# Low-rank gate logits as one fp32r product of stacked parts, and other places and banks for the transposes of the second seam half

## The chip, the cores and the metric

The kernel runs on one core of a Trainium2 chip. The core has five engines with instruction queues of their own: TensorE (PE; its weight loads are listed as PEld), VectorE (DVE), ScalarE (ACT), GpSimd (POOL) and SyncE (SP), which here issues the DMAs. An engine takes its instructions in order and waits at semaphores for the others. The metric is the device time of one execution in microseconds (us); lower is better.

## The reference, cut to what matters

One layer of a hybrid decoder: a gated DeltaNet branch A and a gated linear attention branch B (GLA), merged by gates, an output projection, and an MLP with a squared ReLU. 1024 tokens, model width 1024, all in float32. The two places that the change touches:

```python
h = rms_norm(x, norm_mix_pre[l])
proj = h @ w_in[l]                    # ..., a_b, a_a (4 columns each), ..., b_glr (16 columns), ...
# branch B: decay of each of 512 key channels, from a rank-16 input
gate_logit = gate_lr @ gate_w2 + gate_b
log_a = log_sigmoid(gate_logit) / 16
...
merged = sigmoid(gate_a) * y_a + sigmoid(gate_b) * y_b
x = x + rms_norm(merged @ w_o[l], norm_mix_post[l])
h = rms_norm(x, norm_mlp_pre[l])
u = square(relu(h @ w_mlp_up[l]))
x = x + rms_norm(u @ w_mlp_down[l], norm_mlp_post[l])
```

## The kernel before

**Precision.** Nearly every large product is made of fp32r matmuls. An operand is split into a leading part, rounded to fp32r by a ScalarE copy, and a trailing part, which VectorE makes by subtracting (`split`, L237). A product is then three matmuls: leading by leading, leading by trailing, trailing by leading (`mm3`). Some small products stay in plain float32.

**Stages in order.** A prologue normalises x and writes its transpose as hT and hL. Then comes the DeltaNet stage (pool `cv`), the GLA stage (pool `gl`), the merge of the two branches (pool `mp`), the output projection with the start of the MLP (pool `op`; called the seam below), the MLP's up projection (pool `ml`) and its down projection (pool `dn`). In the first two stages a function `drive` writes down TensorE's order: a main list of large products, and lanes of small jobs that are put in when a clock `T.t`, counted up by every matmul's columns, has reached their time. `TensorClock` (L57 on) counts a plain float32 matmul as four times an fp32r one. The order on the other engines is set by a scheduler with priorities; `tc.high_priority` moves instructions forward.

**Weights** come in slabs of 256 KB. Each is loaded into one of four buffers `w` of the pool `wraw` and split into `wh` and `wl`, of which there are three each.

**The low-rank path.** `decays` computes 24 narrow columns of the projection: 8 for the DeltaNet's beta and decay, 16 for the gate input. Their weights `wx` are held as 128 columns with zeros between: leading parts at columns 0 to 7 and 32 to 47, trailing parts 64 columns further. The result, 112 rows of 1024 tokens, is copied to `sm` in float32. `decays2` transposes rows 0 to 71 of it and computes the DeltaNet's decays. In the GLA stage `gw2` holds gate_w2 twice, at rows 32 to 47 and 96 to 111, zeros elsewhere, and `ball_pair` makes the logits of two heads with four plain float32 products of 128x512 over these 112 rows, into the banks t, l, r, o; there are two such pairs. A linear scan over the logits' log-sigmoid follows.

**PSUM** has four large banks (`gbank`, tag g) and four more with the tags t, l, r, o (`mbank`).

**The seam.** `merged @ w_o` runs in two halves u of 512 tokens, each with two column blocks c of 8 steps (kt). After a half, four row tiles i are normalised one after the other: VectorE writes xt (residual), ScalarE squares it, GpSimd forms the scale rs, VectorE writes m. `turn(u, i)` transposes row tile i in two groups of four and writes parts of the MLP's input: for u = 0 the blocks X11 and X21 and their splits; for u = 1 it writes X12, x22, the split R22, and sums for a Strassen-like scheme of seven products (T1, T2, and what T3 and T4 are made of). In the list of operations the X blocks carry the name `wu`, since they live in buffers of that tag, and T1 to T4 the name `big`.

The turns of u = 0 stand between the steps of the second half's projection (after the steps `TURNS[0]`, counted c * 8 + kt). Those of u = 1 stand in the loop after it, which computes products P1 and P2 of the first eight MLP blocks from the first half alone: 16 steps of 12 matmuls into the banks r and o; a turn comes after each of the steps `TURNS[1]`. Behind this loop `prep(0)` loads weights (L1073) into the buffer that X12 had, T3 and T4 are split, and `early(0)` runs the products P6 (with T2), P7 (T3), P5 (T1), P4 (T4) and P3 of block 0. P6 needs a sum of the weights that prep(0) loads.

```python
TURNS = (2, 5, 6, 9), (3, 6, 10, 12)
...
if step in TURNS[1]:
    turn(1, TURNS[1].index(step))
```

Of the kernel before, what the change touches and what calls it, by code (L numbers as in the profile page):

```python
# [7 lines left out]
F32 = mybir.dt.float32  # L8
F32R = mybir.dt.float32r
U32 = mybir.dt.uint32  # L10
AF = mybir.ActivationFunctionType
ALU = mybir.AluOpType
# [4 lines left out]
P = 128  # L17
S = 1024
# [5 lines left out]
TAU = 16.0  # L24
DFF = 4096
NE = 8
TURNS = (2, 5, 6, 9), (3, 6, 10, 12)
HP = 2000
HPX = 600
HPE = 2000  # L30
# [103 lines left out]
def kernel(  # L134
# [4 lines left out]
    w_mlp_up, w_mlp_down, out, dbg=None,  # L139
):  # L140
    nc = tc.nc
    V, A, G, T, SP = nc.vector, nc.scalar, nc.gpsimd, TensorClock(nc.tensor), nc.sync
# [6 lines left out]
    wraw = ctx.enter_context(tc.tile_pool(name="wraw", bufs=4))  # L149
# [4 lines left out]
    def gbank():  # L154
        return psg.tile([P, 512], F32, tag="g", name="g")
# [3 lines left out]
    def mbank(tag=None):  # L159
        if tag is None:  # L160
            tag = "tlro"[mturn[0] % 4]
            mturn[0] += 1
        return psm.tile([P, 512], F32, tag=tag, name="m" + tag)

    def tt(out, a, b, op, eng=None):
        (eng or V).tensor_tensor(out=out, in0=a, in1=b, op=op)  # L166
# [10 lines left out]
    def act(out, a, func, **kw):  # L177
        A.activation(out=out, in_=a, func=func, **kw)  # L178
# [15 lines left out]
    ident = const.tile([P, P], F32, name="ident")  # L194
# [131 lines left out]
    sgp = tc.alloc_tile_pool(name="sgp", bufs=2, reuse_waits="tile")  # L326
    gp = tc.alloc_tile_pool(name="gp", bufs=1, reuse_waits="tile")

    sm = gp.tile([112, S], F32, name="sm")
    bt = gp.tile([P, NTOK, 8], F32, name="bt")  # L330


# [6 lines left out]
    with tc.tile_pool(name="xp", bufs=3) as xp:  # L339
        pre = []  # L340
        for t in range(NTOK):
# [11 lines left out]
            for g in range(2):  # L353
                pt = mbank()
                for k in range(4):
                    T.transpose(out=pt[:, k * P:(k + 1) * P], in_=xn[:, (g * 4 + k) * P:(g * 4 + k + 1) * P],
                                identity=ident)
# [23 lines left out]
    def decays(cv):  # L381


        ws = cv.tile([P, KT, 24], F32, name="ws", tag="Xc")
        SP.dma_start(out=ws[:, :, 0:8], in_=win[:, :, C_AB:C_AB + 8])
        SP.dma_start(out=ws[:, :, 8:24], in_=win[:, :, C_GLR:C_GLR + 16])
        wx = cv.tile([P, KT, P], F32R, name="wx", tag="Ai", bufs=1)
        with tc.high_priority(offset=HP):
            V.memset(wx.bitcast(F32), 0.0)
            for c, r, n in ((0, 0, 8), (8, 32, 16)):  # L390
                wv = ws[:, :, c:c + n]
                A.copy(out=wx[:, :, r:r + n], in_=wv)
                tt(wx[:, :, r + 64:r + 64 + n], wv, wx[:, :, r:r + n].bitcast(F32), ALU.subtract)
        for u in range(2):
            us = slice(u * 512, u * 512 + 512)
            ps = gbank()
            for kt in range(KT):
                T.matmul(ps, wx[:, kt, :], hT[:, kt, us], start=kt == 0, stop=False)
                T.matmul(ps, wx[:, kt, :], hL[:, kt, us], start=False, stop=kt == KT - 1)
                yield  # L400
            A.copy(out=sm[:, us], in_=ps[0:112, :])

    def decays2():
        for g in range(2):
            yield LAT
            pb = mbank("tl"[g])[:, 0:288].rearrange("p (t c) -> p t c", c=72)
            for t in range(4):
                T.transpose(out=pb[:, t, :], in_=sm[0:72, (g * 4 + t) * P:(g * 4 + t + 1) * P], identity=ident[0:72, 0:72])
            V.tensor_copy(out=bt[:, g * 4:g * 4 + 4, :], in_=pb[:, :, 0:8])
            tt(bt[:, g * 4:g * 4 + 4, :], pb[:, :, 64:72], bt[:, g * 4:g * 4 + 4, :], ALU.add)  # L410
        btb = bt[:, :, 0:4].rearrange("p t h -> p h t")
        bta = bt[:, :, 4:8].rearrange("p t h -> p h t")
        act(beta, btb, AF.Tanh, scale=0.5)
        ts(beta, beta, 0.5, ALU.mult, 0.5, ALU.add)
        tt(yv, bta, bc(dtb, NTOK), ALU.add)
        act(u_, yv, AF.Abs)
        act(u_, u_, AF.Exp, scale=-1.0)
        ts(s_, u_, 2.0, ALU.add)
        V.reciprocal(out=s_, in_=s_)
        tt(s_, s_, u_, ALU.mult)  # L420
        s2 = u_
        tt(s2, s_, s_, ALU.mult)
        ts(pl, s2, 2.0 / 17, ALU.mult, 2.0 / 15, ALU.add)
        for c in (13, 11, 9, 7, 5, 3, 1):
            tt(pl, pl, s2, ALU.mult)
            ts(pl, pl, 2.0 / c, ALU.add)
        tt(pl, pl, s_, ALU.mult)
        ts(yv, yv, 0.0, ALU.max)
        tt(gr, yv, pl, ALU.add)
        tt(gr, gr, bc(nea, NTOK), ALU.mult)  # L430
        grf = gr.rearrange("p h t -> p (h t)")
        yield 10.0
        pg = mbank("t")
        T.matmul(pg[:, 0:32], upper, grf, start=True, stop=True)
        T.matmul(pg[:, 32:64], ones, grf, start=True, stop=True)
        gcf = gc.rearrange("p h t -> p (h t)")
        V.tensor_copy(out=gcf, in_=pg[:, 0:32])
        act(eg, gc, AF.Exp)
        tt(ef, pg[:, 32:64].rearrange("p (h t) -> p h t", t=NTOK), gc, ALU.subtract)
        ts(ef, ef, 0.0, ALU.min)  # L440
        act(ef, ef, AF.Exp)
        act(egl, pg[:, 32:64].rearrange("p (h t) -> p h t", t=NTOK), AF.Exp)
        yield LAT
        pgt = mbank("l")
        T.transpose(out=pgt[0:32, 0:P], in_=gcf, identity=ident)
        grow = wraw.tile([P, 2, 256], F32, tag="w", name="w")[0:32, 0, 0:P]
        V.tensor_copy(out=grow, in_=pgt[0:32, 0:P])
        SP.dma_start(out=d_g, in_=grow)
# [331 lines left out]
    with tc.tile_pool(name="gl", bufs=1, reuse_waits="tile") as gl:  # L780

        reserve(gl, (("gq", 512, 3), ("gk", 512, 3), ("gvh", S, 3), ("gvl", S, 3), ("gr", S, 4)))
        gw2 = gl.tile([112, 512], F32, name="gw2")
        V.memset(gw2, 0.0)
        for r in (32, 96):
            SP.dma_start(out=gw2[r:r + 16, :], in_=gla_gate_w2[0])
        smask = gl.tile([P, 8, 64], F32, name="smask")
        V.memset(smask, 1.0)
        V.memset(smask[:, :, 0:1], 0.0)
# [7 lines left out]
        def ball_pair(hh):  # L797

            lap = ball.rearrange("p h (u i) -> p (h u) i", u=2)
            for n in range(4):  # L800
                h, u = hh + n // 2, n % 2
                yield LAT
                gbias = chan[:, 48 + h:49 + h]
                pl_ = mbank("tlro"[n])
                T.matmul(pl_, gw2[:, h * P:(h + 1) * P], sm[:, u * 512:u * 512 + 512], start=True, stop=True)
                ts(lap[:, n, :], pl_, gbias, ALU.add, 0.0, ALU.min)
                act(e1s[:, n, :], pl_, AF.Abs, bias=gbias)
            act(e1s, e1s, AF.Exp, scale=-1.0)
            act(e1s, e1s, AF.Ln, bias=1.0)
            tt(e1s, lap, e1s, ALU.subtract)  # L810
            for n in range(4):
                V.tensor_tensor_scan(out=lap[:, n, :], data0=smask.rearrange("p c i -> p (c i)"), data1=e1s[:, n, :],
                                     initial=0.0, op0=ALU.mult, op1=ALU.add)
# [156 lines left out]
        for h in range(H):  # L970
            if h % 2 == 0:
                jobs.append(("b%d" % h, [], lambda mark, h=h: ball_pair(h)))
            jobs.append(("m%d" % h, [("v%d" % h, 2.0), ("k%d" % h, 2.0), ("b%d" % (h // 2 * 2), BW if h % 2 == 0 else 0)],
                         lambda mark, h=h: gla_mix(h, mark)))
# [15 lines left out]
    with tc.tile_pool(name="mp", bufs=1, reuse_waits="tile") as mp:  # L990
# [22 lines left out]
        for c in range(4):  # L1013
# [12 lines left out]
            for b in range(2):  # L1026
                for u in range(2):
                    us = slice(u * 512, u * 512 + 512)
# [61 lines left out]
    with tc.tile_pool(name="op", bufs=1, reuse_waits="tile") as op:  # L1090
# [12 lines left out]
        def turn(u, i):  # L1103
            m = msu[u][i]
            il = slice(i * P, i * P + P)
            pv = []
            for g in range(2):
                pt = mbank("tl"[g])
                for k in range(4):
                    T.transpose(out=pt[:, k * P:(k + 1) * P], in_=m[:, (g * 4 + k) * P:(g * 4 + k + 1) * P],  # L1110
                                identity=ident)
                pv.append(pt.rearrange("p (k c) -> p k c", c=P))
            if u == 0:
                for g, n in enumerate(("11", "21")):
                    A.copy(out=X[n][:, :, il], in_=pv[g])
                    hilo(R[n], k4, il, X[n][:, :, il])
            else:
                x11, x21, x12, x22 = (X[n][:, :, il] for n in ("11", "21", "12", "22"))
                A.copy(out=x12, in_=pv[0])
                tt(x22, pv[1], x12, ALU.subtract)  # L1120
                hilo(R["22"], k4, il, pv[1])
                tt(x12, x12, x11, ALU.subtract)
                tt(x11, x22, x11, ALU.add)
                hilo(T2, k4, il, x11)
                hilo(T1, k4, il, x12)
                tt(x21, x21, x11, ALU.subtract)

        for u in range(2):
# [4 lines left out]
            for c in range(2):  # L1133
                banks = [gbank() for _ in range(4)]
                cs = slice(c * 512, c * 512 + 512)
                for kt in range(KT):
                    hi, lo = load_slab512(wov[:, kt, cs], wsp, "w")
                    for i in range(4):
                        il = slice(i * P, i * P + P)
                        mm3(banks[i], mg_[u][0][:, kt, il], mg_[u][1][:, kt, il], hi, lo, kt == 0, kt == KT - 1)  # L1140
                    if u and c * KT + kt in TURNS[0]:
                        turn(0, TURNS[0].index(c * KT + kt))
                with tc.high_priority(offset=HPE):
# [6 lines left out]
            for i in range(4):  # L1150
                t = u * 4 + i
# [84 lines left out]
    with tc.tile_pool(name="ml", bufs=1, reuse_waits="tile") as ml:  # L1236
# [147 lines left out]
        for n in range(NU):  # L1384
# [18 lines left out]
            else:  # L1403
                if n == NU - 1:

                    r = [hp2.tile([P, 8, 512], F32, tag=t, name="r" + t) for t in ("R11", "R21")]
# [131 lines left out]
```

## Time and profile before

| | us |
|---|---|
| median of 3 runs | 1704.4 (1701.24 to 1704.83) |
| the profiled execution | 1699.28 |
| its span in the trace | 1697.5 |

| engine | busy us in the span |
|---|---|
| PE / PEld | 1653.0 / 1403.0 |
| DVE | 987.2 |
| ACT | 771.5 |
| POOL | 135.9 |

On the time axis of the trace the first gate products run at 439.8 us, the second pair's at 647.8, the seam's P1 and P2 steps from 1060.7 on, and P6 of block 0 from 1116.85.

How to read it: a stretch row gives the busy time of each engine in it, with the number of instructions in brackets. In the chain each line is a piece of the work that ended last, with its start and length. In a timeline a bracket at the end of a row tells how long the engine had been idle before it and what released it. A matmul's listed duration overlaps that of the next one, so the pace is read from starts.

### The profile page before, as it was taken

The numbers are of one execution on the slowest core, as the hardware profiler recorded it, in microseconds if no ns is written. First come the engines' busy times: TensorE is split into PE (matmuls) and PEld (weight loads), VectorE is DVE, ScalarE is ACT, GpSimd is POOL, SyncE is SP. The second block draws the span as 40 slices with busy tenths as digits, with TensorE's granted clock in tenths as the row PEclk, the third lists the DMA queues.
The fourth block names the chain that finished last, engine by engine and source line by source line (L and its number), as shares of the span: only waits on it lengthen the run. The fifth ranks groups of instructions, "written<-read, shape, count | busy, mean of one in ns | idle before, by whom it ended". The sixth has DMA issues, their size and how long they took to land.

```text
span 1697.5 us, 24475 instructions
## 1 busy us (share of the span) xinstructions
PE 1653.0 (97%) x9174; PEld 1403.0 (83%) x9174; DVE 987.2 (58%) x1678; ACT 771.5 (45%) x1576; POOL 135.9 (8%) x222
## 2 busy tenths in 40 slices
PE   7999999999999999999999999989999999999997
PEld 6888778878898989998888888778888878888886
DVE  5677565872445335643354545798777655564764
ACT  5456554643533335433421235654555555443442
POOL 3010111111001000001100011200000000000021
PEclk9999999999999999999999999999999999999999
DMA  5222213322211212122743345687678698786763
GB/s 168 56 73 76 84 38 90 92 59 67 79 45 38 69 43 58 38 63 87 235 150 97 111 159 174 212 263 231 205 258 281 240 334 307 243 272 221 249 224 136
DMA packets 186405, 251.39 MB, mean 148 GB/s; under 512 B 23351, under 2 KB 108430, under 8 KB 186286
## 3 DMA queue, kind: packets, MB, share of 16 engines
q1 hardware_dynamic: 186286, 249.83, 45.7%
q8 instruction: 72, 1.18, 0.3%
q14 instruction: 47, 0.39, 0.1%
HBM read 185.79 MB, written 63.98 MB: 147 GB/s over the span
## 4 chain that ended last, share of the span: by engine, by line
PE 82%; DVE 7%; DMA 4%; ACT 4%; issue 2%; POOL 1%; SPq 0%; DVEq 0%; ACTq 0%; POOLq 0%
PE g L68 58%; PE mr L68 8%; PE mo L68 7%; PE ml L68 4%; PE mt L68 3%; DMA gb<-d_g 2%; DVE Xt L166 1%; PE mt L72 1%; DVE Xi L548 1%; DVE wl L166 1%; ACT E L178 1%; DMA oraw<-d_oa 1%; ACT wh L237 0%; DMA rv<-in_w_mlp_down_dram 0%; ACT Zp L604 0%
## 5 line engine op out<-in xcount | busy, mean ns | idle before, releaser
L166 DVE TENSOR_TENSOR wl<-w,wh 128x512 fp32r<-128x512 f32 x181 | 125.6, 695 | 223.5 <-ACT wh L237 220.0
L68 PE MATMUL g<-hT,wh 128*128 128x512 f32 (+1 forms) x600 | 239.1, 399 | 1.2 <-DVE gr L175 0.9
L68 PE MATMUL g<-hL,wh 128*128 128x512 f32 (+1 forms) x600 | 232.8, 388 | 0.0
L68 PE MATMUL g<-hT,wl 128*128 128x512 f32 (+1 forms) x600 | 232.1, 387 | 0.0
L237 ACT CAST wh<-w 128x512 fp32r<-128x512 f32 x184 | 113.8, 619 | 208.0 <-PE g L68 175.0
L68 PE MATMUL g<-wh,hT 128*128 128x256 f32 x640 | 185.7, 290 | 0.0
L68 PE MATMUL g<-wl,hT 128*128 128x256 f32 x640 | 182.1, 284 | 0.0
L68 PE MATMUL g<-wh,hL 128*128 128x256 f32 x640 | 182.0, 284 | 0.0
L68 PE MATMUL g<-big 128*128 128x512 f32 x768 | 175.3, 389 | 1.7 <-ACT big L1231 1.6
L68 PEld LDWEIGHTS g<-big 128*128 128x128 f32 x768 | 144.0, 188 | 32.3 <-ACT big L1231 2.0
L166 DVE TENSOR_TENSOR big<-ru,big 128x1024 fp32r<-128x1024 f32 x53 | 64.9, 1225 | 114.6 <-ACT big L1231 114.2
L68 PEld LDWEIGHTS g<-hT,wl 128*128 128x128 f32 x600 | 113.4, 189 | 21.6 <-DVE wl L166 0.2
L68 PEld LDWEIGHTS g<-hT,wh 128*128 128x128 f32 x600 | 113.4, 189 | 21.5 <-DVE gr L175 1.1
L68 PEld LDWEIGHTS g<-hL,wh 128*128 128x128 f32 x600 | 113.8, 190 | 18.8 <-issue 1.0
L1231 ACT CAST big<-ru 128x1024 fp32r<-128x1024 f32 x53 | 55.8, 1053 | 153.1 <-PE g L68 56.6
L68 PEld LDWEIGHTS g<-wh,hT 128*128 128x128 f32 x640 | 123.1, 192 | 1.4 <-issue 1.0
L68 PEld LDWEIGHTS g<-wl,hT 128*128 128x128 f32 x640 | 123.2, 193 | 1.2 <-issue 1.0
L68 PEld LDWEIGHTS g<-wh,hL 128*128 128x128 f32 x640 | 123.1, 192 | 0.1
L68 PE MATMUL g<-wh,big 128*128 128x512 f32 x256 | 81.1, 393 | 0.2 <-DVE m L166 0.2
L68 PE MATMUL g<-big,wh 128*128 128x512 f32 x256 | 78.8, 389 | 0.0
L178 ACT ACTIVATE c<-c 128x512 f32<-128x512 f32 x104 | 64.1, 630 | 21.8 <-DVE c L166 20.1
L166 DVE TENSOR_TENSOR big<-rv,big 128x1024 fp32r<-128x1024 f32 x53 | 64.6, 1218 | 0.2
(450 smaller groups left out, 3377.1 us busy)
## 6 DMA issues: line engine op xcount, KB each, us to landing
ru<-d_u SPq DMA_DIRECT2D x53, 512.0 KB, 4.6
w<-in_w_in_dram SPq DMA_DIRECT2D x80, 256.0 KB, 2.7
rv<-in_w_mlp_down_dram SPq DMA_DIRECT2D x37, 512.0 KB, 5.4
wu<-in_w_mlp_up_dram SPq DMA_DIRECT2D x32, 512.0 KB, 5.6
d_u<-c SPq DMA_DIRECT2D x56, 256.0 KB, 2.9
d_u<-us SPq DMA_DIRECT2D x48, 256.0 KB, 3.3
us<-in_w_mlp_down_dram SPq DMA_DIRECT2D x48, 256.0 KB, 4.4
xt<-in_x_dram SPq DMA_DIRECT2D x16, 512.0 KB, 5.4
```

The lines of the kernel that those rows point to most:

```text
L68: return self.eng.matmul(out, lhsT, rhs, start=start, stop=stop, skip_group_check=more)
L72: return self.eng.transpose(out=out, in_=in_, identity=identity)
L166: (eng or V).tensor_tensor(out=out, in0=a, in1=b, op=op)
L178: A.activation(out=out, in_=a, func=func, **kw)
L237: A.copy(out=hi, in_=raw)
L548: V.tensor_reduce(out=X[:, :, i:i + 1], in_=tv, axis=AX.X, op=ALU.add)
L1231: A.copy(out=s4[:, i], in_=raw)
```

## The change

`sm` is divided. Rows 0 to 71 go in float32 to a tile in a buffer of the pool `cv` (tag C) that `decays2` reads. All 112 rows go, rounded to fp32r, to `smr`, and rows 64 to 95 of it are then replaced by what the rounding left of them. In `wx` the leading part of the gate columns now stands three times (columns 16, 32, 80) and the trailing part at 96. So `smr` holds for the gate input: leading (16 and 32), its remainder (80), and the small share of the weights' trailing part (96).

`gw2` becomes fp32r with gate_w2 at rows 16, 32, 80 and 96. It is staged in float32 in a buffer of `wraw`, rounded by ScalarE, and rows 0 to 31 are replaced by what the rounding left. The eight gate products then are one fp32r matmul each.

In the seam, the turns move to the steps 2, 4, 6, 8 in both halves, and those of the second half transpose into the four large banks in place of t and l.

```diff
-TURNS = (2, 5, 6, 9), (3, 6, 10, 12)
+TURNS = (2, 4, 6, 8), (2, 4, 6, 8)
...
-    sm = gp.tile([112, S], F32, name="sm")
+    sm = {}
+    smr = gp.tile([112, S], F32R, name="smr")
...
+        sm[0] = cv.tile([72, S], F32, tag="C", name="sm", bufs=2)
...
-            for c, r, n in ((0, 0, 8), (8, 32, 16)):
+            for c, n, rh, rl in ((0, 8, (0,), 64), (8, 16, (16, 32, 80), 96)):
                 wv = ws[:, :, c:c + n]
-                A.copy(out=wx[:, :, r:r + n], in_=wv)
-                tt(wx[:, :, r + 64:r + 64 + n], wv, wx[:, :, r:r + n].bitcast(F32), ALU.subtract)
+                for r in rh:
+                    A.copy(out=wx[:, :, r:r + n], in_=wv)
+                tt(wx[:, :, rl:rl + n], wv, wx[:, :, rh[0]:rh[0] + n].bitcast(F32), ALU.subtract)
...
-            A.copy(out=sm[:, us], in_=ps[0:112, :])
+            A.copy(out=sm[0][:, us], in_=ps[0:72, :])
+            A.copy(out=smr[:, us], in_=ps[0:112, :])
+            tt(smr[64:96, us], ps[64:96, :], smr[64:96, us].bitcast(F32), ALU.subtract)
...
-        gw2 = gl.tile([112, 512], F32, name="gw2")
-        V.memset(gw2, 0.0)
-        for r in (32, 96):
-            SP.dma_start(out=gw2[r:r + 16, :], in_=gla_gate_w2[0])
+        gw = wraw.tile([P, 2, 256], F32, tag="w", name="w").rearrange("p a c -> p (a c)")[0:112]
+        gw2 = gl.tile([112, 512], F32R, name="gw2")
+        V.memset(gw, 0.0)
+        for r in (16, 32, 80, 96):
+            SP.dma_start(out=gw[r:r + 16, :], in_=gla_gate_w2[0])
+        A.copy(out=gw2, in_=gw)
+        tt(gw2[0:32], gw[0:32], gw2[0:32].bitcast(F32), ALU.subtract)
...
-                T.matmul(pl_, gw2[:, h * P:(h + 1) * P], sm[:, u * 512:u * 512 + 512], start=True, stop=True)
+                T.matmul(pl_, gw2[:, h * P:(h + 1) * P], smr[:, u * 512:u * 512 + 512], start=True, stop=True)
...
-                pt = mbank("tl"[g])
+                pt = gbank() if u else mbank("tl"[g])
```

More of the change, by code (lines that the diff above doesn't have):

```diff
@@ L407, in decays2 @@
             for t in range(4):
-                T.transpose(out=pb[:, t, :], in_=sm[0:72, (g * 4 + t) * P:(g * 4 + t + 1) * P], identity=ident[0:72, 0:72])
+                T.transpose(out=pb[:, t, :], in_=sm[0][:, (g * 4 + t) * P:(g * 4 + t + 1) * P], identity=ident[0:72, 0:72])
             V.tensor_copy(out=bt[:, g * 4:g * 4 + 4, :], in_=pb[:, :, 0:8])
```

## The prediction

> **What bounds the kernel now.** I read the page first, then the table of stretches, then the chain of work that ended last, then the timelines of single engines where the chain leaves TensorE.
>
> ```profile
> PE 1653.0 (97%) x9174; PEld 1403.0 (83%) x9174; DVE 987.2 (58%) x1678; ACT 771.5 (45%) x1576; POOL 135.9 (8%) x222
> PE 82%; DVE 7%; DMA 4%; ACT 4%; issue 2%; POOL 1%; SPq 0%; DVEq 0%; ACTq 0%; POOLq 0%
> ```
>
> TensorE is busy 97% of the span and is 82% of the chain. So time leaves in two ways only: fewer TensorE cycles, or fewer TensorE waits. The change tries one of each. Where they would act is seen in stretches of 20 us (columns: stretch, length, then busy us of PE, PEld, DVE, ACT, POOL; granted clock; DMA share; GB/s):
>
> ```profile
> 440.00:460.00 20.00, 20.00 (x82) 15.19 (x81) 9.00 (x10) 11.10 (x13) 0.59 (x1) 1.00 0.23 66
> 640.00:660.00 20.00, 20.00 (x149) 18.07 (x149) 7.19 (x11) 10.14 (x15) 0.00 (x0) 1.00 0.22 69
> 1080.00:1100.00 20.00, 17.58 (x79) 14.34 (x78) 14.60 (x23) 12.68 (x25) 0.88 (x2) 0.91 0.56 179
> 1100.00:1120.00 20.00, 15.33 (x65) 11.95 (x64) 18.20 (x27) 14.93 (x25) 0.00 (x0) 0.87 0.64 206
> 1120.00:1140.00 20.00, 20.00 (x86) 16.48 (x85) 17.95 (x30) 7.74 (x13) 0.00 (x0) 0.95 0.88 273
> ```
>
> The gate logits fall into the first two stretches: TensorE never idles there, so each of its cycles counts. The second seam half falls into 1080 to 1120: here TensorE is idle for 7.1 us and its clock drops. The chain there (start, length, what; the lines left out between 1108 and 1117 are issue time of 0.02 to 0.05 us):
>
> ```profile
> 1063.56 2.72 PE mo L68 x12
> ...
> 1071.72 0.44 PE mt L72 x4
> 1072.16 0.44 PE ml L72 x4
> ...
> 1082.88 0.61 DVE R L166
> ...
> 1083.63 0.63 PE ml L72 x4
> 1084.26 4.34 PE mo L68 x12
> ...
> 1107.20 1.75 DVE big L166 x2
> 1108.94 0.02 SPq L1073
> ...
> 1109.02 0.38 SPq L1073
> ...
> 1109.44 5.26 DMA wu<-in_w_mlp_up_dram
> ...
> 1114.73 0.70 DVE ss L166
> ...
> 1115.46 0.70 DVE ss L166
> ...
> 1116.18 0.63 ACT wh L237
> ...
> 1116.85 5.48 PE mr L68 x12
> 1122.33 0.69 PE g L68 x3
> ```
>
> A step of the seam is 12 matmuls, 2.72 us (0.227 each); a turn is eight transposes, 0.88. The chain leaves TensorE twice. **First wait:** turn 1 of the half needs bank l, and VectorE frees it late with R. **Second wait:** product P6 of the first MLP block needs a weight load that may only start when VectorE has written the last T1 of turn 3 (the load goes into the tile of X12). TensorE's own rows give the lengths:
>
> ```profile
> 1083.63 0.63 PE L72 MATMUL ml<-ident,m 128*128 128x128 f32 x4 [2.42 <-DVE R L166]
> 1116.85 1.22 PE L68 MATMUL mr<-big,wh 128*128 128x512 f32 x2 [4.67 <-ACT wh L237]
> 1083.60:1087.80 4.20, 4.17 (x14) 3.38 (x15) 4.17 (x7) 2.16 (x4) 0.00 (x0) 0.59 0.75 231
> 1116.80:1122.20 5.40, 5.35 (x13) 3.83 (x14) 5.40 (x10) 2.11 (x5) 0.00 (x0) 0.54 1.10 368
> ```
>
> Behind both waits the granted clock is about half (0.59, 0.54). So the first costs 2.42 + (4.34 - 2.72) = 4.04 us, the second 4.67 + (5.48 - 2.72) = 7.43.
>
> **The change, part by part.** *Gate logits.* Eight products of 128x512 over 112 rows, recorded as two matmuls each:
>
> ```profile
> L68 PE MATMUL mt<-sm,gw x4: 590/591/594, 439.8 to 648.2; 112*128 112x512 f32 x4
> 647.92 0.86 PE mt L68 x2
> ```
>
> Each occupies 0.86 us of the chain. In fp32r the nearest row is the seam's matmul, 0.227 for the same 512 columns. Ends: 0.227 (gain 8 x 0.633 = 5.1 us) and 0.86 (gain 0). I take 0.227, since every fp32r row of 512 columns in the seam stands there. The order on TensorE is worked out with the same shorter duration, so nothing else moves past it.
>
> *What the new operands need.* The rows below show where this lies: the logit copies (L401), and the gate weights (L784, L786) before the first product at 439.8.
>
> ```profile
> 53.49 0.59 ACT L401 COPY sm<-g 112x512 f32<-112x512 f32 x1 [2.88 <-PE g L68]
> 59.06 0.62 ACT L237 CAST wh<-w 128x512 fp32r<-128x512 f32 x1 [4.00 <-PE g L68]
> L72 PE MATMUL mt<-ident,sm x4: 225/226/227, 57.4 to 57.6; 72*128 72x72 f32 x4
> 428.89 0.48 DVE L784 MEMSET gw<- 112x512 f32 x1
> 430.28 0.91 SPq L786 DMA_DIRECT2D gw<-in_gla_gate_w_dram  x2
> DMA to landing us min/median/max: 2.4/2.5/2.7
> ```
>
> Two more ScalarE copies (0.59 each), two VectorE subtracts (at most 0.69, as for 128 rows) and two small casts: ScalarE idles 4.00 us before 59.06, the copy that the transposes at 57.4 need ends at 54.1, so 3.3 us of delay is free. The logit banks stay taken about 1.3 us longer, and the next product reaches them some 4 us after it starts (18 of its matmuls). I count 0; without the cover it is 0.59 + 0.69 for the last half. Gate weights: memset, now four loads on SP (0.45 each), a cast on ScalarE and a subtract on VectorE. Even starting as late as now: 430.3 + 1.8 + 2.5 + 0.6 + 0.7 = 435.9, ahead of 439.8 by 3.9 us. Behind the waiting cast stand ScalarE's weight casts of the first k slabs. I count 0, and at worst 1 us, should the cast queue behind them. The staging tile also takes one of the four weight slots for about 7 us; every slab load then moves by one slab, 5.4 us, against three slots left. Count 0.
>
> *Turns of the first half* (step 5 to 4, 9 to 8): the same eight transposes, 0.88, and none of TensorE's waits lies there. They hide beside nothing and cost the same at any step. 0; a wait for rows that come too late would be the price, and the seam below shows how large such a one is.
>
> *Turns of the second half.* They go from after steps 3, 6, 10, 12 to after 2, 4, 6, 8. Without waits they then fall at 1069.0, 1075.3, 1081.7 and 1088.0 (step ends 1063.56 + 2.72 a step, 0.88 a turn). They need the normalised rows m:
>
> ```profile
> 1064.69 1.29 DVE L175 SCALAR_TENSOR_TENSOR m<-xt,rs,wpre 128x1024 f32<-128x1024 f32 x1 [0.71 <-POOL rs L186]
> 1080.99 1.29 DVE L175 SCALAR_TENSOR_TENSOR m<-xt,rs,wpre 128x1024 f32<-128x1024 f32 x1 [0.71 <-POOL rs L186]
> 1082.80 0.68 DVE L166 TENSOR_TENSOR R<-ml,R 128x512 fp32r<-128x512 f32 x1
> 1083.40 0.68 DVE L166 TENSOR_TENSOR wu<-wu 128x512 f32<-128x512 f32 x1
> ```
>
> First and last of four: rows ready at 1066.0 and 1082.3, so 5.4 us apart, at 1066.0, 1071.4, 1076.8, 1082.3. Each is 3 to 5.7 us ahead of its new turn. With four large banks, turn 2 needs only the banks of turn 0, transposed 12 us earlier; so the first wait goes: 4.04.
>
> For the second wait VectorE decides. A turn is seven VectorE operations, 0.60 apart (1082.80, 1083.40); each step also takes one split of 0.60 in 2.72, 22% of VectorE. Turn 0 fits into the gaps of the row chain. From 1082.3 three turns are left: 21 x 0.60 / 0.78 = 16.2, so the last T1 stands at 1098.5. From there the chain above takes 1108.94 to 1116.85 = 7.9 to the first P6 matmul: ready at 1106.4. TensorE gets there at 1088.0 + 0.88 + 7 x 2.72 = 1107.9. No wait, 1.5 us in hand. ScalarE has four operations of 0.6 a turn, less than VectorE. On SP, the load now comes ahead of the stores of the last steps; three buffers stand behind those. T3 and T4 follow on VectorE, four subtracts of double width (about 4 x 1.2), before P7 at 1110.6.
>
> Sum for the seam: now 1063.56 to 1122.33 = 58.8; then 15 x 2.72 + 4 x 0.88 + 2.72 = 47.0; so 11.7. (The two waits alone make 11.5; the turns' edges the rest.) Since only 1.5 us are in hand, I take 0.7 off: **11.0**. All told 5.1 + 11.0 = **16.1 us**. What follows is bound by TensorE, with loads in step with it, so it moves along. The profiled execution took 1699.28 us (span 1697.5 and 1.8 around it): 1683.2 by this sum. The runs' median is 1704.4, 5.1 above; from there **1688.4**.
>
> **The rivals.**
>
> *VectorE still ends last.* For: it is busy 18.2 of 20 us in 1100 to 1120. If it idles between turns as now, T1 stands at about 1103 and P6 waits 3 us, and 1.6 more at the low clock: gain 5.1 + 7.1, 1692.2. Against: in the rows above it idles ahead of m for GpSimd (0.71 each), and the earlier turns give it work to put there. [...]
>
> *GpSimd is held up by the turns.* The row chain passes two GpSimd steps per row, and three more prepare the next:
>
> ```profile
> 1059.88 0.19 POOL L172 TENSOR_SCALAR rs<-rs 128x1 f32<-128x1 f32 x1
> 1060.94 1.29 POOL L172 TENSOR_SCALAR rs<-rs 128x1 f32<-128x1 f32 x1
> ```
>
> The same step takes 0.19 or 1.29, the latter beside VectorE's 1.28 us row operation. If each of the five waits for one turn operation of 0.69, a row takes 5.4 + 3.5 = 8.9; the last is ready at 1092.7, turns 2 and 3 wait 2.1 and 2.6, and with 1.6 of low clock the seam gains 5.4: 1693.9. Against: two of the five are on the path, and that alone (1.4 a row) stays inside the slack. [...]
>
> *The logits' gain is absorbed* by a wait further on in its stage that now ends last: 1693.4. Against: TensorE is busy for all 20 us of both stretches.
>
> *The new places do nothing at the end of the seam:* the load stays late by as much as TensorE comes earlier. Only the logits count: 1699.3.
>
> *Slower.* VectorE takes its operations in order; if the turns' stand ahead of the row operations, the rows come late and TensorE stands at each turn. Each row behind a full turn (4.2) and held GpSimd steps (3.5) takes 13.1; to be slower by 3.4 us, P6 has to end at 1122.3 + 5.1 + 3.4 = 1130.8, so the last turn has to come 2.72 + 1.6 + 7 x 2.72 + 0.88 earlier, at 1106.6: a row period of 13.5. At 14 it is 1709. Against: now the R of turn 0 (1082.80), whose transposes ran at 1072, stands behind the last row (1080.99): rows go first.
>
> **How the numbers follow.** Forecast 0.60; VectorE last 0.16; GpSimd 0.07; absorbed 0.05; no effect at the seam 0.07; slower 0.05. About 0.2% (3.4 us) is what a measurement of this kernel can tell from no change, and the runs shown spread by 3.6. The range reaches from 1682.5 (the full 11.7, and a run 5.1 below the median as the profiled one) to 1699.0, which holds the first four cases. Faster: the first four and half of the fifth, 0.91; same 0.04; slower 0.05.
>
> **What would show it.** Gate matmuls at 0.23 us with no wait for gw; no wait over 0.5 us at the transposes of the half; the first load of L1073's step issued before 1101 on the old time axis; granted clock 1.00 from 1080 to 1120. A wait of TensorE for m says the rows are late; one for wh at P6, that VectorE is. I am wrong at the root if the time moves by under 8 us, or if TensorE waits at a place that it does not wait at now.

## The result, and the profile after

| | before | after |
|---|---|---|
| median of the runs taken side by side (4 each) | 1704.39 us | 1693.21 us (1691.42 to 1693.99) |
| ratio, 95% interval | | 0.9937, 0.992 to 0.9954 |
| the profiled execution | 1699.28 | 1693.49 |
| its span | 1697.5 | 1691.8 |

The kernel became faster, by 11.2 us where 16 was forecast; the time lies inside the range, 4.8 above the forecast. The two profiled executions differ by 5.7 only. Three later runs took 2034.5 and 3310.5 us (logits_only) and 2036.0 (places_only), far from all others: they count in the medians of the table of runs below, not in its ratios. The trace says where the gain was made and where it went. First the page of after: the engines' busy time and their shares of the chain.

```profile
PE 1647.6 (97%) x9166; PEld 1400.3 (83%) x9166; DVE 987.2 (58%) x1681; ACT 772.6 (46%) x1581; POOL 134.8 (8%) x222
PE 81%; DVE 8%; DMA 5%; ACT 4%; issue 2%; POOL 1%; SPq 0%; DVEq 0%; ACTq 0%; POOLq 0%
```

The busy time of TensorE fell by 5.4 us, about what the logits were to save, but that agreement is luck: busy time also counts the stretches at half clock, of which this trace of before has more (13.65 us up to its last matmul, that of after 6.83), and between before_again and after_again it fell by 2.1 only (1650.5 to 1648.4). In the chain DMA grew from 4% to 5%. The list of instructions that touch `gw` shows the logits (shortest/median/longest ns, first and last start):

```profile
L68 PE MATMUL mt<-smr,gw x2: 395/396/396, 440.5 to 646.0; 112*128 112x512 f32 x2
L796 ACT CAST gw<-w x1: 609/609/609, 430.0 to 430.0; 112x512 fp32r<-112x512 f32 x1
L166 DVE TENSOR_TENSOR gw<-w,gw x1: 679/679/679, 430.7 to 430.7; 32x512 fp32r<-32x512 f32 x1
```

One matmul where there were two, and the weights are ready at 431.4, 9 us ahead. Then the stretches of the second seam half, columns as before:

```profile
1080.00:1100.00 20.00, 18.89 (x84) 14.60 (x84) 19.93 (x31) 17.25 (x31) 0.00 (x0) 1.00 0.57 178
1100.00:1120.00 20.00, 17.64 (x77) 13.94 (x75) 15.38 (x26) 8.79 (x15) 0.00 (x0) 1.00 1.01 314
```

The granted clock is 1.00 now (0.91 and 0.87 before), but TensorE still idles 3.5 us of these 40, and VectorE is busy for 19.93 of 20 us. TensorE's timeline tells for whom it waits; these are all the waits that it marks from the half's start on to 1125:

```profile
1078.12 0.73 PE L68 MATMUL mo<-R,wh 128*128 128x512 f32 x2 [0.57 <-ACT e L1198]
1085.15 0.73 PE L68 MATMUL mo<-R,wh 128*128 128x512 f32 x2 [0.42 <-ACT e L178]
1094.54 0.72 PE L68 MATMUL mr<-R,wh 128*128 128x512 f32 x2 [0.69 <-ACT e L178]
1107.76 0.72 PE L68 MATMUL mr<-big,wh 128*128 128x512 f32 x2 [1.76 <-ACT e L178]
1120.72 0.73 PE L68 MATMUL g<-big,wh 128*128 128x512 f32 x2 [1.32 <-DVE c L166]
```

Nothing waits at a transpose. The waits are for ScalarE's evacuations `e` of banks r and o, a releaser that the profile before did not show here. P6 (1107.76) is 9.1 us earlier than before, and it runs at full clock, so the next product starts at 1110.62 against 1122.17: 11.55 us are won by here.

They do not last. The next place where TensorE stops is the start of the down projection. Three answers on after follow, one to a fence: the chain of waits, TensorE's timeline, and a stretch behind it.

```profile
1382.05 7.66 DMA rv<-in_w_mlp_down_dram
1389.72 0.02 issue
1389.74 1.05 ACT big L1242
```

```profile
1390.84 11.35 PE L68 MATMUL g<-big 128*128 128x512 f32 x36 [3.49 <-ACT big L1242]
```

```profile
1391.00:1397.00 6.00, 6.00 (x15) 4.64 (x16) 5.81 (x5) 5.06 (x5) 0.00 (x0) 0.50 1.00 393
```

And the same of before, its timeline and its stretch:

```profile
1398.96 3.37 PE L68 MATMUL g<-big 128*128 128x512 f32 x12 [1.62 <-ACT big L1231]
```

```profile
1399.00:1405.00 6.00, 5.94 (x25) 4.61 (x26) 5.83 (x5) 4.95 (x5) 0.00 (x0) 1.00 1.05 417
```

The wait grew from 1.62 to 3.49, and behind it the clock is now at half for 6 us (15 matmuls where there were 25). So the gain goes 11.55 (after P6), 8.12 (1398.96 to 1390.84), 5.7 (the span).

### The profile page after: what moved, and what is told of

It is laid out like the page before. It is cut to its first block, busy times and chain, and to the rows that moved or that the text cites. A ratio compares the mean times of both kernels' runs of the same rounds, so it can differ in the third digit from the quotient of the medians.

```text
span 1691.8 us, 24460 instructions
## 1 busy us (share of the span) xinstructions
PE 1647.6 (97%) x9166; PEld 1400.3 (83%) x9166; DVE 987.2 (58%) x1681; ACT 772.6 (46%) x1581; POOL 134.8 (8%) x222
## 4 chain that ended last, share of the span: by engine, by line
PE 81%; DVE 8%; DMA 5%; ACT 4%; issue 2%; POOL 1%; SPq 0%; DVEq 0%; ACTq 0%; POOLq 0%
PE g L68 59%; PE mr L68 7%; PE mo L68 6%; PE ml L68 4%; PE mt L68 3%; DMA gb<-d_g 2%; DVE Xt L166 1%; PE mt L72 1%; DVE Xi L555 1%; DVE wl L166 1%; DMA xt<-in_x_dram 1%; ACT E L178 0%; DMA rv<-in_w_mlp_down_dram 0%; DVE big L166 0%; DMA wu<-in_w_mlp_up_dram 0%
```

## The experiments

Of each run the table gives the median and the ratio to runs of the kernel before that were taken with it on the same chip (its median was 1700.81, 1700.25 and 1700.57 in the three sets). The ratio decides.

| run | median us | ratio, 95% interval |
|---|---|---|
| before_again | 1700.35 | 0.9997, 0.9989 to 1.0006 |
| logits_only | 1697.81 | 0.998, 0.997 to 0.999 |
| seam_only | 1696.0 | 0.9974, 0.9966 to 0.9983 |
| places_only | 1695.02 | 0.9964, 0.9951 to 0.9977 |
| banks_only | 1698.42 | 0.999, 0.998 to 1.0 |
| before_hoist | 1697.23 | 0.9982, 0.9972 to 0.9991 |
| after_again | 1691.1 | 0.9948, 0.9933 to 0.9962 |
| p6_own_bank | 1691.48 | 0.9942, 0.9927 to 0.9958 |
| swap | 1686.48 | 0.9921, 0.9907 to 0.9935 |
| hoist | 1686.9 | 0.9924, 0.991 to 0.9938 |
| swap_hoist | 1683.89 | 0.9901, 0.9887 to 0.9914 |
| swap_hoist_tl | 1686.29 | 0.9909, 0.9894 to 0.9924 |

From each trace's timeline of TensorE I took the same marks, all in us: the start of the half's first product, P6 counted from there, the start of the down projection counted from P6 and the wait in it, and from there to the end of the span.

| run | half starts | P6 after it | down projection after P6 | wait in that | to the end |
|---|---|---|---|---|---|
| before | 1060.67 | 56.2 | 282.1 | 1.62 | 298.5 |
| before_again | 1059.65 | 54.5 | 282.3 | 1.79 | 298.6 |
| logits_only | 1053.15 | 57.0 | 285.1 | 4.25 | 300.9 |
| banks_only | 1059.19 | 53.4 | 284.1 | 3.57 | 300.0 |
| places_only | 1059.75 | 51.4 | 282.5 | 3.70 | 299.9 |
| seam_only | 1059.67 | 51.1 | 283.1 | 3.86 | 300.9 |
| after | 1055.68 | 52.1 | 283.1 | 3.49 | 301.0 |
| after_again | 1056.41 | 51.4 | 283.0 | 3.17 | 300.0 |
| p6_own_bank | 1053.01 | 50.4 | 286.6 | 4.37 | 300.4 |
| swap | 1053.45 | 49.4 | 281.3 | 2.57 | 299.6 |
| hoist | 1056.43 | 51.8 | 280.7 | 1.26 | 298.4 |
| before_hoist | 1061.35 | 55.0 | 281.7 | 1.47 | 298.6 |
| swap_hoist | 1055.63 | 48.9 | 281.9 | 2.75 | 298.4 |
| swap_hoist_tl | 1055.67 | 52.1 | 280.4 | 2.08 | 299.7 |

With the new logits the half starts at 1054.9 on the mean of eight traces, without them at 1060.0 on six; single traces lie up to 2 us off these means.

The last column falls into three groups by the time for which the clock in the trace stands at half behind the wait: not at all in five traces (298.4 to 298.6), 3.41 us in five (299.6 to 300.0), 6.83 us in four (300.4 to 301.0). So what is lost behind the wait is the clock. (In the trace of swap the granted clock reads 0.95 where others read 1.00, though 16 matmuls run in 3.41 us as elsewhere; it is not compared here.)

### The parts of the change alone

**before_again** is the kernel before, unedited.

> The kernel before, unchanged, to see how its executions differ among themselves. Theory A (the half clock): the 5 us between its profiled execution (1699.3) and its median (1704.4) are pieces of time at half clock, above all behind the wait at the start of the down projection; so its executions at 1704 show a lower mean granted clock than 0.994, and a profile of one shows a half-clock piece there. Rival B (loads): they differ by longer landings there at the same mean clock. By either the ratio to before is 1.000.

**logits_only** is the kernel before with the gate product of the change and all that it needs; of its edit the product is shown:

```diff
-                T.matmul(pl_, gw2[:, h * P:(h + 1) * P], sm[:, u * 512:u * 512 + 512], start=True, stop=True)
+                T.matmul(pl_, gw2[:, h * P:(h + 1) * P], smr[:, u * 512:u * 512 + 512], start=True, stop=True)
```

> The fp32r gate product alone, turns as before. Theory A: TensorE's axis moves by 8 x 0.63 = 5.1 us at the gate products and keeps it to the seam, so about 1699 against 1704. Rival: the start of the down projection, where TensorE waits for loads, takes it back; then the axis still shows 5 us less at the seam and under 2 less at the end.

**seam_only** is the kernel before with the new places and banks, **places_only** with the places alone:

```diff
-TURNS = (2, 5, 6, 9), (3, 6, 10, 12)
+TURNS = (2, 4, 6, 8), (2, 4, 6, 8)
...
-                pt = mbank("tl"[g])
+                pt = gbank() if u else mbank("tl"[g])
```

> Places and banks of the turns alone, gate product in float32. Theory A: the seam is shorter by about 6.7 us on TensorE's axis (as in the changed kernel) and the median falls by 5 to 7. Rival (the two parts share one gain): under 3.

> Only the turns' places change; they stay in banks t and l. Theory A: the wait at P6 shrinks by the earlier load, but turn 2 or 3 waits for bank l, as turn 1 did before (2 us or more, with half clock possible), so 2 to 4 us less gain than seam_only. Rival (banks do not matter, as the turns are 6 us apart now): the same as seam_only within 1 us.

The kernel before repeats itself (0.9997), with the same waits at bank l and P6 in its trace; what its runs say of the clock stands in the last section. The logits win 5 us up to the seam but only 0.002 in the end (3.4 us, by the interval 1.7 to 5.1), between what the theory and the rival said: at the down projection the wait is 4.25 instead of 1.8, with the clock at half for 6.83 us behind it. The seam alone wins 0.0026 (4.4 us, 2.9 to 5.8), again between the two. Its P6 comes 3.4 us (against before_again) or 5.1 (against before) earlier and, unlike theirs, runs at full clock (2.87 us to the product behind it, 5.42 and 5.32 in theirs), so that the product behind P6 comes 5.9 or 7.5 earlier; again a wait of 3.86 stands at the down projection. The two ratios together make 0.9954, beside 0.9948 for the whole: the parts add up, and in the traces each pays at the same late place.

places_only is no slower than seam_only, as the rival said; I had expected 2 to 4 us less gain. In its trace TensorE has one wait in the half before P6, and none at P6:

```profile
1078.75 0.63 PE L72 MATMUL ml<-ident,m 128*128 128x128 f32 x4 [2.29 <-DVE R L166]
```

A stretch there shows the clock:

```profile
1080.10:1083.50 3.40, 3.40 (x10) 2.71 (x9) 3.40 (x5) 1.38 (x3) 0.00 (x0) 0.54 1.05 308
```

So bank l still costs 2.29 and a piece of low clock, and P6 comes when it does in seam_only, where P6 waits 1.56 for `e` instead. Two bounds end within 0.3 us of each other; taking one away exposes the other.

### The banks alone

**banks_only** is the kernel before with `gbank()` in the second half and the old places.

> The kernel before with one part of the change: the second half's transposes go to the four large banks, at the old places, with the old gate product. Theory (TensorE's two waits in the half are not two prices: product P6 starts when its load and VectorE's chain behind it are ready, whatever TensorE did ahead of it, and turns at the old places leave that chain late): the 2.4 us wait for bank l at turn 1 goes, the wait of 4.5 to 4.7 us for wh at P6 grows to 6 to 7, P6 starts 54 to 57 us after the half's first product as before, and the median is within 1.5 us of the kernel before. Rival (the prediction's sum): bank l's wait and its low clock go and P6's wait stays, so P6 starts 50.5 to 53 us after the half's start and the median is 3 to 4.5 us lower.

Bank l's wait is gone and P6's is what it was, as the rival said; P6, at 53.4, and the time lie between the two expectations, and nearer to my theory. TensorE's timeline:

```profile
1112.57 1.22 PE L68 MATMUL mr<-big,wh 128*128 128x512 f32 x2 [4.50 <-ACT wh L237]
```

P6 comes 1.1 us earlier than in before_again, 2.8 than in before, and 1.7 us (0.999) are left at the end, by the interval 0 to 3.4. In the prediction this first wait was worth 4.04.

### What stands ahead of P6

**after_again** is the changed kernel, unedited, on the chip of the next three runs.

> The changed kernel once more, unedited, beside the kernels before and the variants of it on one chip; what the variants gain is read against its median. Theory: the change wins 5.1 us in the gate logits and about 6.7 us in the seam, all of it is there when the first MLP block starts, and some 3 to 5 us are given back at the start of a down projection (the join). Expected: a ratio of 0.992 to 0.995 (8 to 13 us), in its profile a wait of TensorE of 1.8 us (1.5 to 2.2) at P6 for bank r, waits of 0.4 to 0.7 in the turns for the evacuations e, and over 3 us at the join with the granted clock near 0.5 behind it. Rival (the profiled run of the changed kernel was an odd one): the wait at the join is 1.6 to 1.9 as in the kernel before, and the ratio is below 0.992.

It came as expected, with 3.17 at the down projection. Here the change is worth 0.0052, 8.8 us.

**p6_own_bank** gives P6 another bank:

```diff
-            a, c, d = mbank("ro"[n % 2]), gbank(), gbank()
+            a, c, d = mbank("t" if n == 0 else "ro"[n % 2]), gbank(), gbank()
```

> The changed kernel with one edit: the first product of the first MLP block (P6) takes bank t instead of bank r, which the seam's last product has only just filled. Theory (TensorE stands at P6 because bank r is freed behind a cast that waits in ScalarE's queue): the 1.76 us wait for e goes; what is then late is the weight half wl, whose operation ended only about 0.6 us before the wait does, so P6 starts 0.5 to 1.3 us earlier. If the start of the down projection gives back what the seam wins, the median stays within 1 us of the changed kernel's; if it does not, it is 0.5 to 1.3 us lower. Rival (the wait stands for VectorE's late T1, the bank only happened to come last): P6 waits for ss or wl instead, at the same time within 0.3 us.

Its timeline of TensorE:

```profile
1104.19 0.50 PE L68 MATMUL mt<-big,wl 128*128 128x512 f32 x1 [0.16 <-DVE wl L166]
...
1117.37 0.73 PE L68 MATMUL g<-big,wh 128*128 128x512 f32 x2 [1.97 <-DVE c L166]
```

P6 starts 1.0 us sooner (1.7 against the first run of after), as the theory said, is caught by the weight half `wl` at once, and 13 us later a wait of 1.97 for VectorE's `c` (none in after_again) takes back more than that. The time does not change. Bank r was the last of several things that end close together there: it held up P6 by a microsecond, and within the noise nothing of that reaches the end.

**swap** turns round two operations of a turn:

```diff
                 A.copy(out=x12, in_=pv[0])
-                tt(x22, pv[1], x12, ALU.subtract)
                 hilo(R["22"], k4, il, pv[1])
+                tt(x22, pv[1], x12, ALU.subtract)
```

> The changed kernel with one edit: in a turn, R22 is written before X22 is subtracted, so that ScalarE's and VectorE's readings of one bank stand in another order. Theory (the small waits of the turns, 0.57, 0.42, 0.69 and the ScalarE waits of 0.7 to 1.0 before them, come from ScalarE's cast R<-g waiting for VectorE to have done with the same bank, which puts ScalarE's evacuations late): at least two of those three waits go and the last T1 of turn 3 stands within 0.3 us of where it was; P6 starts up to 1.5 us earlier. Rival (ScalarE's queue is late for another reason, the weight casts in it): the waits stay within 0.3 us of what they are. Time: within 1.5 us of the changed kernel's by both, lower by the theory.

Here my theory fell. The three waits in the turns stay (0.23, 0.61, 0.52), about as the rival said. But the time falls by 4.6 us, three times what either allowed, and at P6 there is no wait at all: counted from the half's start, P6 comes 2.0 us sooner than in after_again, and the product behind it 3.4, since with the wait of 1.86 the low clock behind it has gone (from P6 to that product 2.93 us, 4.31 in after_again). Between the first load for P6 and P6 after takes 13.3 us, swap 8.7. In SP's timeline of after, the second load stands behind a store whose operand ScalarE has just made; in that of swap, both loads go at once:

```profile
1094.45 0.38 SPq L1084 DMA_DIRECT2D wu<-in_w_mlp_up_dram  x1
1095.55 0.32 SPq L1203 DMA_DIRECT2D d_u<-e  x1
1095.92 1.36 SPq L1084 DMA_DIRECT2D wu<-in_w_mlp_up_dram  x2
```

```profile
1093.39 0.32 SPq L1203 DMA_DIRECT2D d_u<-e  x1
1094.17 1.01 SPq L1084 DMA_DIRECT2D wu<-in_w_mlp_up_dram  x2
```

The second difference is on ScalarE, whose order the edit changed too. In after, the relu that empties bank r stands behind three casts, in swap ahead of them:

```profile
1105.47 0.62 ACT L237 CAST wh<-ss 128x512 fp32r<-128x512 f32 x1 [4.09 <-DVE ss L166]
1106.07 0.62 ACT L1257 CAST wh<-wu 128x512 fp32r<-128x512 f32 x1
1106.59 0.61 ACT L237 CAST wh<-ss 128x512 fp32r<-128x512 f32 x1
1107.11 0.59 ACT L178 ACTIVATE e<-mr 128x512 f32<-128x512 f32 x1
```

```profile
1100.75 0.60 ACT L178 ACTIVATE e<-mr 128x512 f32<-128x512 f32 x1 [1.54 <-DMA d_u<-e]
1101.54 0.62 ACT L237 CAST wh<-ss 128x512 fp32r<-128x512 f32 x1 [0.18 <-DVE ss L166]
```

Counted from the half's start, swap issues the first load 1.9 us later than after (40.7 against 38.8) and yet starts P6 2.7 us sooner. What is late in the changed kernel is the chain behind the load, not VectorE's last T1. Which of the two differences counts for how much no run separates, and why the scheduler placed the relu and the store differently I did not follow up.

### What takes the gain back

**hoist** raises the priority of the first loads of the down projection:

```diff
-            u, v = load(pool, "ru", d_u[b][:, j:j + 2, :]), load(pool, "rv", src(j))
+            with tc.high_priority(offset=HP if p == "P1" else 0):
+                u, v = load(pool, "ru", d_u[b][:, j:j + 2, :]), load(pool, "rv", src(j))
```

> The changed kernel with one edit far behind the seam: the loads of the first product of each MLP block's down projection (ru and rv) are put ahead in SP's order. Theory (what logits and seam win is given back at the start of the down projection, where the first operands come back from memory by a fixed chain of store, load and cast, and where the wait is long enough for the clock to go to half): the wait of 3.5 us there falls below 1.5, no half clock stands behind it, and the median is 3 to 7 us below the changed kernel's (the wait and the 3.4 us that the low clock costs). Rival (what is late there is VectorE's and ScalarE's part, not the loads): the wait stays within 1 us of what it is and so does the time. Second rival (the loads ahead hold up the stores that the last products need): the wait grows, and the time by 1 to 4 us.

Its chain of waits and its timeline of TensorE:

```profile
1382.61 5.26 DMA rv<-in_w_mlp_down_dram
```

```profile
1388.99 13.36 PE L68 MATMUL g<-big 128*128 128x512 f32 x56 [1.26 <-ACT big L1243]
```

The wait is 1.26, the matmuls behind it run at full clock (1.00 from 1389 to 1393, 16 matmuls in these 4 us), and the median is 4.2 us below after_again. Why is simpler than my theory: the stores still go first, and only one load, that of `wpost`, has moved behind. With it ahead, rv takes 6.9 to 7.7 us to land in all ten traces without the edit; with it behind, 5.1 to 6.6 in four.

**before_hoist** is the same edit on the kernel before.

> The kernel before, without any part of the change, with the loads of ru and rv put ahead in SP's order as in the run hoist. Theory (the changed kernel comes to the start of the down projection with its first loads no earlier than its stores allow, so that the wait there grew from 1.7 to over 3 us and trips the low clock; without the change there is little to win there): the wait of 1.6 to 1.8 at the start of the down projection goes below 0.8, and the median falls by 0.5 to 2 us only. Rival (the loads ahead are worth the same 4 us with or without the change, so the change did not create that loss): 3.5 to 5 us lower.

It won 0.0018 (3.1 us, by the interval 1.5 to 4.8), between the two expectations. rv lands in 5.11 us there, but the profiled wait is still 1.47: the loads left SP 1.4 us later after P6 than in before_again. The mean granted clock of its eleven runs is 0.996 against 0.9945 in 61 runs of the kernel before, which is about 2.5 of the 3.1 us; in which places the unprofiled runs lost it is not seen. So the loss at the down projection was partly there before the change; that the change made all of it is refuted.

### Both together

> The changed kernel with both edits of the runs swap and hoist. Theory (they take away two different losses: swap puts the relu that frees bank r ahead of the weight casts on ScalarE, so P6 starts about 2 to 2.6 us sooner, and hoist takes the join's wait and its low clock): P6 starts 49 to 50 us after the half's first product, the join's wait is under 2 us, and the median is 3 to 5 us below that of each alone (1682 to 1684 beside 1686.5 and 1686.9). Rival (both work on the same loss at the join, and the one leaves nothing for the other): 1685 to 1687.

> The run swap_hoist with the second half's transposes put back into the two small banks t and l; gate product and places stay as changed. Theory (the places alone did the seam's part, the four large banks nothing, as places_only was no slower than places and banks together): the median within 1 us of swap_hoist's, though a wait of about 2 us for bank l may stand at turn 1, since VectorE's chain to P6 ends no earlier without it. Rival (with P6's own waits taken away TensorE is the bound again, and bank l's wait counts): a wait of 1.5 to 2.5 us for bank l and a median 1.5 to 4 us above swap_hoist's.

**swap_hoist** has both edits and is the fastest version, 16.8 us (0.9901) below the kernel before, where swap alone makes 13.4 and hoist alone 12.9: the two losses are different ones, though not quite additive: against my expectation a wait of 2.75 is back at the down projection, this time without low clock. **swap_hoist_tl** puts the transposes back into banks t and l. Its P6 comes 3.2 us later, with the old wait in TensorE's timeline:

```profile
1080.95 0.63 PE L72 MATMUL ml<-ident,m 128*128 128x128 f32 x4 [2.29 <-DVE wu L166]
```

So by the trace the large banks do count once P6 no longer waits for its own operands. In the time the intervals of the two overlap; four runs each do not settle it.

## Why the prediction was right in direction and too large in size

**Gate logits, 5.1: right.** From the first to the fourth product of a group TensorE's timeline of before takes 6.74 us (439.76 to 446.50), that of after 4.84 (440.49 to 445.33): 0.63 a product, eight times, as the sum had it:

```profile
439.76 1.02 PE L68 MATMUL mt<-sm,gw 112*128 112x512 f32 x2
...
446.50 1.02 PE L68 MATMUL mo<-sm,gw 112*128 112x512 f32 x2
```

```profile
440.49 0.40 PE L68 MATMUL mt<-smr,gw 112*128 112x512 f32 x1
...
445.33 0.40 PE L68 MATMUL mo<-smr,gw 112*128 112x512 f32 x1
```

The half starts 5.1 us earlier on the mean of all traces. That the pair of profiles gives 4.99 (1060.84 to 1055.85 in the chains of waits) is partly luck, since the stages ahead of the gates differ by 0.7 us in it.

**Their operands and weights, 0: right.** No wait for `gw` or `smr`; the rows stand above.

**Turns of the first half, 0: right, as far as the traces show.** places_only and seam_only have them with the old gate product, and start the second half at 1059.75 and 1059.67, before_again at 1059.65.

**Rows in time, and GpSimd not held up: right.** The list of VectorE's row operations and TensorE's timeline, both of after:

```profile
L175 DVE SCALAR_TENSOR_TENSOR m<-xt,rs,wpre x4: 1283/1284/1285, 1059.7 to 1076.6; 128x1024 f32<-128x1024 f32 x4
```

```profile
1083.70 1.03 PE L72 MATMUL g<-ident,m 128*128 128x128 f32 x8
```

The last row is ready at 1077.9, 5.8 us ahead of its turn, and no transpose waits.

**First wait, 4.04: it went, but it was no price of its own.** places_only keeps it and loses nothing by it beside seam_only; banks_only removes it and keeps 1.7 us. The prediction added it to the second wait, while in the main each decides only when the other is out of the way.

**Second wait, 7.43 with its clock: here a term was mis-sized.** The prediction put it thus: "From there the chain above takes 1108.94 to 1116.85 = 7.9 to the first P6 matmul: ready at 1106.4." Its start was nearly right: the load leaves at 1094.45, on the old axis (plus 4.99) 1099.4, against 1098.5 for the T1 that frees the buffer. But the chain took 13.3 us, because at the new time it runs amid the rest of the seam. From the first load's issue to VectorE's first sum: 8.55 instead of 5.8, of which 7.06 is the landing of the second load (5.26 before). Between the sums: 1.75 instead of 0.7, since a subtract of T stands between them. From the cast to P6: 2.3 instead of 0.7, for bank r. After's chain has the landing, VectorE's timeline the sums:

```profile
1095.92 7.06 DMA wu<-in_w_mlp_up_dram
```

```profile
1103.00 0.69 DVE L166 TENSOR_TENSOR ss<-wu 128x512 f32<-128x512 f32 x1 [2.20 <-DMA wu<-in_w_mlp_up_dram]
1103.62 1.22 DVE L166 TENSOR_TENSOR big<-wu,big 128x1024 fp32r<-128x1024 f32 x1
1104.75 0.68 DVE L166 TENSOR_TENSOR ss<-ss,wu 128x512 f32<-128x512 f32 x1
```

0.9 us late at the start and 5.4 in the chain, less the 1.5 in hand, make 4.8; P6 came at 1107.76 plus 4.99, or 1112.75, against 1107.9. The seam so won 6.6 (11.55 less 4.99) and not 11.0.

TensorE itself was late too. It had reached P6 at 1106.0, on the old axis 1111.0, where the prediction has 1107.9; the three waits for `e` make 1.68 of these 3.1 us. Here the prediction put ScalarE at nothing: "ScalarE has four operations of 0.6 a turn, less than VectorE." So even with the chain in time P6 would have come late. The test is swap: with a chain of 8.7 and no wait at P6, P6 stands 49.4 us after the half's start, between the 52.1 of after and the 47.0 of the prediction's sum.

By one of its own signs the prediction was wrong at the root: "or if TensorE waits at a place that it does not wait at now". The waits for `e` in the half (0.57, 0.42, 0.69) and the 1.32 for `c` behind P6 stand at such places. The other signs came as it said: the first load left before 1101 on the old axis, the clock was 1.00, no transpose waited.

**What follows, 0: wrong.** "What follows is bound by TensorE, with loads in step with it, so it moves along." Up to the down projection 3.4 us were given back: 1.9 in its wait, 1.3 in the new wait for `c` behind P6, 0.2 elsewhere; 2.4 more behind it at the low clock. There, 282 us behind the edit, store, load and cast follow one another, and the trace of before showed the 1.62 us wait as the next place at which TensorE is not the bound.

Why that wait grew is seen only in part. It is the landing of rv and a cast of 1.05, less the time by which rv left SP before TensorE ran out of work. This lead is 6.84 us in before and 6.53 in before_again, and 4.2 to 5.4 in the other twelve traces. Of the 1.87 in the pair, the lead makes 1.54 and the landing 0.32. The chains of before and of after, one fence each, show that an earlier load, rR, took longer to land too (rv of after stands above):

```profile
1375.56 4.82 DMA rR<-d_u
1390.50 7.34 DMA rv<-in_w_mlp_down_dram
```

```profile
1365.61 6.47 DMA rR<-d_u
```

But the wait does not follow what was won ahead of it: banks_only, whose product behind P6 comes only 1.2 us earlier than in before_again, has a lead of 4.9 and a wait of 3.57. What makes these loads late stays open.

**The sum.** For the two profiles 4.99 + 6.56 - 3.43 - 2.42 = 5.70, against 16.1. The medians differ by more, 11.2 of 16.0, since the profiled run of before was a quick one; but that median of 1704.4 was itself high: 61 later runs of the kernel before average 1700.4, and beside them the change is worth about 9 us, little more than half of the forecast. That the time lies inside the range owes as much to its width of 16.5 us as to the sum. (By its own terms, 1683.2 and 5.1, the forecast should read 1688.3.)

**The rivals.** Three of them gave times within about 1 us of the measured one (1692.2, 1693.9, 1693.4), so the time alone picks none. The first, that VectorE's chain still ends last, came nearest in mechanism, though not for the reason it gave: VectorE did not idle between turns, it was full (19.93 of 20), and load and ScalarE were late with it. That the logits' gain is absorbed by a later wait came true in part, not in its own stage but at the down projection. GpSimd's delay and "slower" did not happen, nor did "nothing at the end of the seam", where 6.6 us were won.

## What to carry to other kernels

When two waits of one engine lie on one path, work out when each operand is ready with the other wait gone; do not add them. A chain of load, sum, cast that took 8 us in a gap takes 13 amid the work that it is moved into: count again every queue that it passes, stores on SP and casts on ScalarE among them. And before a gain is carried to the end, look in the trace for the next place where the bound engine waits, however short and however far: there part of the gain can be lost again.

## What the runs showed of the hardware

**Behind a wait of 2 to 3 us the clock stood at half in some traces and at full in others.** In the first profile of before the wait of 2.42 us at bank l was followed by a stretch at half clock; in before_again the same wait, 2.54 us there, was not. One fence each, before first:

```profile
1084.40:1087.80 3.40, 3.40 (x10) 2.67 (x9) 3.37 (x6) 1.87 (x4) 0.00 (x0) 0.52 0.74 230
```

```profile
1083.00:1086.40 3.40, 3.40 (x18) 2.83 (x17) 3.37 (x7) 2.62 (x5) 0.00 (x0) 1.00 0.66 195
```

In the same 3.4 us ten matmuls run in the one and eighteen in the other. In after_again the clock is at half behind the 1.86 us wait at P6, in swap_hoist at full behind one of 2.75:

```profile
1109.00:1112.40 3.40, 3.40 (x10) 2.61 (x9) 3.40 (x7) 1.90 (x4) 0.00 (x0) 0.50 0.80 227
```

```profile
1386.50:1390.50 4.00, 3.95 (x16) 2.95 (x17) 3.80 (x4) 3.26 (x4) 0.00 (x0) 1.00 0.95 369
```

Up to the last matmul, the low stretches of before start at 128.54, 1084.27 and 1114.99 us and last 3.41, 3.41 and 6.83; after has one, from 1390.19, of 6.83. The length of a wait alone does not tell whether a low stretch follows, as 1.86 and 2.75 show; what decides it was not shown.

**A lower mean clock goes with longer runs, and with much of the spread.** Of the 61 runs of the kernel before, those with a mean granted clock of 0.993 average 1702.6 us (11 runs), 0.994: 1700.7 (18), 0.995: 1700.3 (22), 0.996: 1697.9 (9); one stands at 0.997. A thousandth of the clock is 1.7 us of the span of 1697.5, as much as 3.41 us at half clock cost. The 61 runs reach from 1695.9 to 1705.0, so a single profile, before or after, can stand some microseconds off by chance, and a term read from the clock behind one wait is not sure to be there in the next run.
